# A lead of 224 bytes ahead of all pools of the on-chip memory

## The chip, the cores and the metric

One core of a Trainium2 chip. The metric is the device time of one execution in microseconds, as the median of several runs; lower is better. Each of the core's engines (TensorE, VectorE, ScalarE, GpSimd, SyncE) has its own queue of instructions and they wait for one another by semaphores. Sixteen DMA engines move data between the device's main memory and the on-chip memory (128 partitions; an address below is a byte within a partition, the same in all of them).

## The reference

One inference step of a decoder layer: a matrix-memory branch (mLSTM) and a sliding-window attention branch side by side, merged by gates, with an adaptive norm in front and a final norm. It runs on a prompt of 1024 tokens and on 8 samples of 4 tokens with states and caches. Cut to its main lines, from `layer`, `mlstm_chunk` and `sink_attend`:

```
h = rmsnorm(x, g_norm) * (1 + scale) + shift            # scale, shift, gate = silu(c) @ w_ada + b_ada
(mq, mk, mv, mi, mf, mo, mz, aq, ak, av, az, gm, ga) = split_in(h @ w_in)
# mLSTM branch, chunks of 128 tokens, 4 heads:
s = (q @ k.T) * exp(dmat - m_hat)
num = s @ v + w_inter * (q @ C);  C_new = decay * C + (w_end * k).T @ v
y_m = norm(num / max(|dot|, exp(-m_hat))) * sigmoid(mo) * silu(mz)
# attention branch, window of 128, 8 heads over 2 key heads, with sinks:
p = exp(q @ k.T / 8 - mx);  o = p / (sum(p) + exp(sink - mx)) @ v
y_a = o * silu(az)
u = sigmoid(gm) * (y_m @ w_mo) + sigmoid(ga) * (y_a @ w_ao)
y = rmsnorm(x + gate * (u @ w_o), g_final)
```

Everything is float32. D_MODEL is 1024, the input projection has 5896 columns, and the states, the last keys and values and both outputs are returned.

## The kernel before

The kernel is one program for one core, written by the function `body`. The token axis (1024 + 32) is cut into pieces of 384, 384 and 288 columns, or into halves of 512. Activations are kept transposed, channels on the 128 partitions.

**Start.** `load_x` loads x by channel block: eight tiles of 128 x 512 for each half of the tokens (`x<-xT` in the profile, rows of 2048 bytes a partition), with a tile `small` of constants and samples in between. ScalarE and VectorE square each tile as it lands (`xsq<-x`), TensorE sums the squares (`xs`), and from the sums come the factors of the norm (`xb`). Meanwhile parts of w_ada come in as `early_h`, `early_l` and `adar_q`, from which TensorE works out scale and shift.

**Middle.** Each float32 product of an activation with a weight is made of three products of halves in a reduced format: h is split into `h_h` + `h_l`, a weight tile into `wh` + `wl`, and TensorE adds `wh*h_h`, `wh*h_l` and `wl*h_h`. The jobs `g_ak`, `g_av`, `g_aq`, `g_mq`, `g_mk`, `g_mv` do this for the projections by pieces of 384 or 288 columns; `bw`, `bx`, `by`, `bz` for the gates by 512 columns; `g_w_mo` and `foW` to `foZ` for the output projections. In these products the activation is the moving operand and the weight is loaded into the array ahead (`PEld` in the profile), except in `fo`, where parts of w_out (`wo_...`) move and the tokens are loaded.

A class `Side` fits the attention units (`sc`, `pt`, `oT`) and the chunks of the memory branch (`S`, `U`, `n`, with the running state in the tiles `C`) between these jobs by costs written out in the code, and every instruction of TensorE, VectorE and ScalarE stands in a fixed order. Loads and stores are issued by SyncE in the order of the code, a few by ScalarE and GpSimd. Results that have to change their layout go through main memory (`kD`, `qD`, `oD`, `yaD`, `tmD`, `nmd` and others).

**End.** The last product is added to the rows of x, normalised (`rows_h`, `fy`) and stored (`y_p<-rows_h`).

**Places.** Tiles come from two pools of the on-chip memory, `cp` (lines 176 and 307 on: constants and small tiles) and `sp` (line 177: all else). A pool hands out its tiles one after the other, each rounded up to 32 bytes, and `sp` stands behind `cp`. In `sp` the tag `half` (`ht`, line 193) has 50 buffers of 2048 bytes; `wr`, `wh` and `wl` are weight tiles of 2048 bytes; the activations h and y lie in quarters of 4 x 1056 elements, so that one channel block starts 4224 bytes after the one before.

```
        cp = ctx.enter_context(tc.tile_pool(name="cp", bufs=1))
        sp = ctx.enter_context(tc.tile_pool(name="sp", bufs=1))
...
        def ht(shape, name, dt=F32):
            return sp.tile(shape, dt, tag="half", bufs=50, name=name)
...
        cst = cp.tile([128, C_END], F32, name="cst")
        vec = cp.tile([128, 28], F32, name="vec")
```

Of the kernel before, what the change touches and what calls it, by code (L numbers as in the profile page):

```python
# [10 lines left out]
F32 = mybir.dt.float32  # L11
# [23 lines left out]

C_ID, C_S9, C_TRI, C_CM, C_AM, C_TS, C_CS, C_RS, C_S32, C_BM, C_S64 = 0, 128, 137, 265, 393, 649, 681, 713, 745, 777, 785
C_END = 849


def shape_constants():  # L40
    f = np.float32
    c = np.zeros((128, C_END), f)
    i = np.arange(128)
# [129 lines left out]
def body(tc, a):  # L173
    nc = tc.nc
    with ExitStack() as ctx:
        cp = ctx.enter_context(tc.tile_pool(name="cp", bufs=1))
# [16 lines left out]
        def ht(shape, name, dt=F32):  # L193
            return sp.tile(shape, dt, tag="half", bufs=50, name=name)
# [46 lines left out]
        def dma(out, in_, late=False):  # L241
            stores(in_.tensor)
            issue(out, in_, late)
# [52 lines left out]
        def load_x(p, k0, k1, ts):  # L296
            for k in range(k0, k1):
                ts.append(ht([128, 512], f"x{p}_{k}"))
                dma(ts[-1], a["xT"][:, p, k])
# [4 lines left out]
        issue(small, a["small"])  # L304
        load_x(0, 2, KT, xT[0])
        load_x(1, 0, KT, xT[1])
        cst = cp.tile([128, C_END], F32, name="cst")
        vec = cp.tile([128, 28], F32, name="vec")
        cT, xS = (small[:, o:o + KT * n].rearrange("p (k n) -> p k n", k=KT) for o, n in ((C_TRI + 28, 9), (C_TRI + 28 + KT * 9, NS)))
# [2007 lines left out]
def build(d):  # L2317
    nc = bacc.Bacc("TRN2", target_bir_lowering=False, num_devices=1, dynamic_dma_scratch_size=1024)
    aps = {}
    for k, v in d.items():  # L2320
        aps[k] = nc.dram_tensor(k, v.shape, mybir.dt.from_np(v.dtype), kind="ExternalInput").ap()
    for k, s in OUTS.items():
        aps[k] = nc.dram_tensor(k, s, F32, kind="ExternalOutput").ap()
    with tile.TileContext(nc) as tc:
        body(tc, aps)
    return nc
# [19 lines left out]
```

## Time and profile before

| | |
|---|---|
| median of 3 runs | 842.34 us (842.21 to 842.41) |
| the profiled execution | 842.49 us, span 840.7 us, mean granted clock 0.997 |
| busy: TensorE, its weight loads | 819.6 us (97% of the span), 666.8 us (79%) |
| busy: VectorE, ScalarE, GpSimd | 599.2 us (71%), 421.7 us (50%), 66.2 us (8%) |
| moved by DMA | 153.96 MB in 106690 packets, mean 183 GB/s |

The profile is of one execution. Times of rows are in microseconds unless marked ns. "x12" is the number of instructions in a row, `out<-in` names what is written and read, and what stands in brackets or behind an arrow is the idle time ahead and who ended it. The DMA share is of 16 engines and can pass 100% where packets overlap. Rows of the matmuls overlap too, since they are pipelined: what one costs is read from an unbroken piece of many.

### The profile page before, as it was taken

How to read it: one execution, taken by the hardware profiler on the slowest of the kernel's cores; microseconds unless marked ns; L12 is line 12 of the kernel's file. 1: busy time of each engine (PE TensorE's matmuls, PEld its weight loads, DVE VectorE, ACT ScalarE, POOL GpSimd, SP SyncE). 2: the span in 40 equal slices, each digit the busy share in tenths (PEclk: the TensorE clock that was granted, in tenths of full speed). 3: DMA queues.
4: the chain of work that ended last, by engine and by line, in shares of the span. 5: the costliest groups of instructions: out<-in, count | busy, mean ns of one | idle time of the engine just before them, and what ended most of it. 6: DMA issues, size and time to landing. Idle time of an engine off the chain costs nothing.

```text
span 840.7 us, 15062 instructions
## 1 busy us (share of the span) xinstructions
PE 819.6 (97%) x5129; PEld 666.8 (79%) x5129; DVE 599.2 (71%) x1501; ACT 421.7 (50%) x1032; POOL 66.2 (8%) x128
## 2 busy tenths in 40 slices
PE   6999999999999999999999999999999999999996
PEld 3779897888788788887788877777777779997775
DVE  4889886656655555656657776787878988974776
ACT  5664365655475464445464545344545654334342
POOL 0120000000000000000000100000002104250000
PEclk9999999999999999999999999999999999999998
DMA  9997756356445333579735433553345685643532
GB/s 334 374 355 232 201 184 202 117 155 210 138 135 170 104 115 93 179 247 321 261 131 186 139 124 118 166 177 127 126 149 189 210 288 183 205 138 127 200 108 106
DMA packets 106690, 153.96 MB, mean 183 GB/s; under 512 B 20449, under 2 KB 54369, under 8 KB 106581
## 3 DMA queue, kind: packets, MB, share of 16 engines
q1 hardware_dynamic: 100964, 142.25, 51.9%
q10 hardware_dynamic: 4176, 6.56, 2.2%
q0 software_dynamic: 1472, 4.20, 1.3%
q8 instruction: 40, 0.66, 0.3%
q14 instruction: 38, 0.30, 0.1%
HBM read 109.22 MB, written 44.75 MB: 183 GB/s over the span
## 4 chain that ended last, share of the span: by engine, by line
PE 88%; DMA 5%; DVE 4%; issue 1%; ACT 1%; SPq 0%; DVEq 0%; ACTq 0%
PE bw L258 11%; PE bx L258 11%; PE by L258 10%; PE g_aq L258 6%; PE g_w_mo L258 6%; PE bz L258 5%; PE g_mq L258 3%; PE foW L258 3%; PE foX L258 3%; PE foY L258 2%; PE sc L258 2%; PE oT L258 2%; PE foZ L258 2%; PE smp L258 2%; PE pt L263 2%; PE n L258 2%
## 5 line engine op out<-in xcount | busy, mean ns | idle before, releaser
L219 ACT ACTIVATE p<-p,nmx 128x256 f32<-128x256 f32 (+1 forms) x64 | 31.0, 485 | 10.6 <-DVE nmx L219 10.3
L258 PE MATMUL g_aq<-h_h,wh_aq 128*128 128x384 f32 (+1 forms) x96 | 32.5, 338 | 0.0
L219 DVE CUSTOM_DVE_ANT_0 p<-sc,cst,sink 128x256 f32<-128x256 f32 (+1 forms) x64 | 26.2, 464 | 8.3 <-PE sc L258 8.2
L258 PE MATMUL g_w_mo<-ym_l,wh_w_mo 128*128 128x384 f32 (+1 forms) x96 | 31.1, 324 | 0.0
L258 PE MATMUL g_aq<-h_l,wh_aq 128*128 128x384 f32 (+1 forms) x96 | 31.0, 323 | 0.0
L258 PE MATMUL g_w_mo<-ym_l,wl_w_mo 128*128 128x384 f32 (+1 forms) x96 | 31.0, 323 | 0.0
L258 PE MATMUL g_aq<-h_h,wl_aq 128*128 128x384 f32 (+1 forms) x96 | 31.0, 323 | 0.0
L258 PE MATMUL g_w_mo<-ym_h,wh_w_mo 128*128 128x384 f32 (+1 forms) x96 | 31.0, 323 | 0.0
L246 POOL DMA_DIRECT2D oD<-uqv x16 | 8.8, 552 | 202.5 <-ACT uqv L219 172.8
L219 ACT ACTIVATE et<-et,an 128x128 f32<-128x128 f32 x32 | 11.2, 395 | 25.7 <-DVE et L219 21.3
L258 PEld LDWEIGHTS g_aq<-h_h,wh_aq 128*128 128x128 f32 x96 | 18.1, 188 | 2.6 <-issue 1.5
L219 DVE COPY p<-pt 128x512 f32<-128x512 f32 (+1 forms) x16 | 10.5, 655 | 12.3 <-PE pt L263 12.3
L258 PE MATMUL sc<-ukv,uqv 64*128 64x256 f32 (+1 forms) x128 | 18.3, 390 | 0.8 <-DVE p L219 0.8
L258 PEld LDWEIGHTS g_aq<-h_l,wh_aq 128*128 128x128 f32 x96 | 18.1, 188 | 0.0
L258 PEld LDWEIGHTS g_w_mo<-ym_h,wh_w_mo 128*128 128x128 f32 x96 | 18.0, 188 | 0.0
L258 PEld LDWEIGHTS g_w_mo<-ym_l,wh_w_mo 128*128 128x128 f32 x96 | 18.0, 188 | 0.0
L219 ACT ACTIVATE p<-p,den 128x256 f32<-128x256 f32 (+1 forms) x32 | 14.4, 491 | 7.3 <-DVE den L219 7.3
L258 PEld LDWEIGHTS g_aq<-h_h,wl_aq 128*128 128x128 f32 x96 | 18.0, 188 | 0.0
L258 PEld LDWEIGHTS g_w_mo<-ym_l,wl_w_mo 128*128 128x128 f32 x96 | 18.0, 188 | 0.0
L219 DVE TENSOR_TENSOR wor<-wor,gb 128x512 f32<-128x512 f32 x16 | 10.8, 690 | 9.8 <-DMA wor<-w_out 9.7
L258 PE MATMUL g_mq<-h_h,wh_mq 128*128 128x384 f32 (+1 forms) x48 | 16.9, 351 | 0.3 <-ACT mk L219 0.3
L219 ACT ACTIVATE sq<-rows_h 128x512 f32<-128x512 f32 (+2 forms) x14 | 8.2, 583 | 17.8 <-issue 12.0
(2078 smaller groups left out, 2858.7 us busy)
## 6 DMA issues: line engine op xcount, KB each, us to landing
x<-xT SPq DMA_DIRECT2D x16, 256.0 KB, 5.4
early_h<-w_ada SPq DMA_DIRECT2D x8, 512.0 KB, 9.0
adar_ga<-w_ada SPq DMA_DIRECT2D x16, 256.0 KB, 4.3
wr_ga<-w SPq DMA_DIRECT2D x16, 256.0 KB, 2.9
wr_gm<-w SPq DMA_DIRECT2D x16, 256.0 KB, 3.5
taD<-gt SPq DMA_DIRECT2D x16, 256.0 KB, 2.0
tmD<-gt SPq DMA_DIRECT2D x16, 256.0 KB, 4.4
wor<-w_out SPq DMA_DIRECT2D x16, 256.0 KB, 6.6
```

Source lines behind the costliest of these rows:

```text
L219: ins = f(*args, **kw)
L246: ins = (eng or nc.sync).dma_start(out, in_)
L258: in_order(nc.tensor.matmul(out, lhsT, rhs, start=start, stop=stop, skip_group_check=more))
L263: in_order(nc.tensor.transpose(out, in_, idn))
```

## The change

Ahead of the first tile of `cp`, a tile of 56 float32 per partition (224 bytes) is asked for. Nothing writes or reads it.

```diff
 C_END = 849
+LEAD = 56
...
         load_x(1, 0, KT, xT[1])
+        cp.tile([128, LEAD], F32, name="lead")
         cst = cp.tile([128, C_END], F32, name="cst")
```

All tiles of both pools begin 224 bytes later. The places of some, from the allocation lists of the two built programs (first byte, and its distance past a multiple of 256):

```
tile                        before         after
cst (constants)              1152  128      1376   96
one                          5728   96      5952   64
x, first half, block 0      16928   32     17152    0
wr_ak                      119328   32    119552    0
early_h                    137760   32    137984    0
wh_ak                      188704   32    188928    0
h_l, channel block 0       205088   32    205312    0
h_l, channel block 1       209312  160    209536  128
C, its six buffers         222272 to 224992 (64, 96, 128, 160, 192, 224)
                           222496 to 225216 (32, 64, 96, 128, 160, 192)
```

Of the 1491 places of tiles on the chip 1486 move, all by 224; 1255 then begin on a multiple of 256, and 1254 of them began 32 bytes past one. The order of the instructions on every engine and their number are the same. The tiles in the matrix unit's result memory and in main memory stay where they are.

## The prediction

> **What bounds the kernel now.** I read the page first, for the shares of the engines over the span.
>
> ```profile
> span 840.7 us, 15062 instructions
> PE 819.6 (97%) x5129; PEld 666.8 (79%) x5129; DVE 599.2 (71%) x1501; ACT 421.7 (50%) x1032; POOL 66.2 (8%) x128
> ...
> PEclk9999999999999999999999999999999999999998
> DMA  9997756356445333579735433553345685643532
> ```
>
> TensorE is busy for 97% of the span at nearly full granted clock. That leaves 840.7 - 819.6 = 21.1 us without a matmul. The DMA engines are full only in the first slices. The second view is the list of waits, for TensorE alone: what does it wait for in those 21 us?
>
> ```profile
> PE xc L258 <- ACT xsq L219: 6.4, 1, 6.4
> PE S L258 <- DVE C L219: 1.4, 1, 1.4
> PE bw L258 <- DVE wor L219: 0.8, 1, 0.8
> ```
>
> One wait of 6.4 us at the very start, and then nothing over 1.4 us. The rest of the 21 us is mostly the end, behind the last matmul. So a change of addresses can move the time in three places: at the start, where the first matmuls hang on loads; at the end, where the last rows are normalised and stored; and inside the 5129 matmuls, if the place of an operand changes what one of them takes. The third view is the timeline of the start.
>
> ```profile
> 1.65 0.43 SPq L246 DMA_DIRECT2D small<-small  x1
> 2.12 8.90 SPq L246 DMA_DIRECT2D x<-xT  x14
> 5.93 0.42 ACT L219 ACTIVATE xsq<-small 128x256 f32<-128x256 f32 x1 [3.91 <-DMA small<-small]
> 10.04 0.63 ACT L219 ACTIVATE xsq<-x 128x512 f32<-128x512 f32 x1 [0.73 <-DMA x<-xT]
> 10.70 2.06 DVE L219 TENSOR_TENSOR xsq<-x 128x512 f32<-128x512 f32 x3 [0.66 <-DMA x<-xT]
> 12.53 0.58 ACT L219 COPY xsum<-xs 128x512 f32<-128x512 f32 x1 [1.87 <-PE xs L258]
> 13.02 3.74 ACT L219 ACTIVATE xsq<-x 128x512 f32<-128x512 f32 x6
> 17.78 1.49 PE L258 MATMUL xb<-xdg,one 128*128 128x128 f32 x10
> ```
>
> The squares of the first half of x wait for each load in turn, until the last of them starts at 10.70 us. From 13.02 us ScalarE does six squares back to back (3.74 us for 6, with no wait in the row), so there the loads no longer lead. What a load saves by 10.70 us is saved by all that follows; what it saves later is not.
>
> **The change, part by part.** No instruction is added, taken out or moved: the order on each engine is word for word that of before, apart from buffers' numbers. The unused tile of 224 bytes is placed ahead of all others, and every tile of the two pools starts 224 bytes later. The large ones began 32 bytes past a multiple of 256 and now begin on one. Distances between tiles stay as they were. The allocation lists of the two built programs show this for 1486 of 1491 places; the five that stay are four constants and a scratch area. A rival in which the change does nothing to the addresses is thereby out.
>
> *Transfers.* What does a row of a transfer cost, and how much of that can hang on its first address? Two stretches at full load, one of rows of 2048 bytes (x), one of 4096 (w_ada), each with the DMA view:
>
> ```profile
> DMA packets 639, 1.16 MB, mean 386 GB/s; under 512 B 73, under 2 KB 73, under 8 KB 639
> q1 hardware_dynamic: 639, 1.16, 103.1%
> ```
>
> ```profile
> DMA packets 554, 2.03 MB, mean 406 GB/s; under 512 B 60, under 2 KB 60, under 8 KB 553
> q1 hardware_dynamic: 553, 2.02, 102.1%
> ```
>
> The first is 8 to 11 us, with 639 - 73 = 566 large packets in 103.1% of 16 engines x 3 us: 87.4 ns each. The second is 26 to 31 us, with 553 - 60 = 493 in 102.1% of 16 x 5 us: 165.7 ns each. So 2048 bytes more cost 78.3 ns, and about 9 ns of a row are fixed. A row that begins 32 bytes late touches one block of 256 bytes more. All it can gain is the fixed part, 9 ns of 87 (10%); it need not gain anything. I take the price of the 32 bytes that stick out, 78.3 x 32 / 2048 = 1.2 ns (1.4%), because the second 2048 bytes, with their eight block borders, run at the plain rate: a border as such is not dear.
>
> The Trainium skill (DMA: Bandwidth & Descriptors, "How a descriptor splits into AXI transactions") has a row that starts off a multiple of 256 begin with a transaction at the border below. By it a row of 2048 bytes goes from 9 transactions and 65 beats to 8 and 64, an estimate of 1.5% from that page's figures. Its price alone would take the start 0.1 us down, as mine does. No run so far has large rows that start on a multiple, so the trace cannot confirm it.
>
> At the start, the loads that lead run from 2.12 to 10.70 us, 8.6 us. 1.4% of that is 0.12 us; the ends are 0 and 10%, 0.9 us. Later loads are waited for by VectorE and ScalarE alone:
>
> ```profile
> DVE et L219 <- DMA et<-nmd: 13.3, 6, 4.5
> DVE wor L219 <- DMA wor<-w_out: 9.7, 6, 4.0
> ACT wh_w_mo L219 <- DMA wr_w_mo<-w_mo: 7.1, 3, 4.2
> ```
>
> These 30 us are fifteen waits for whole transfers of some 4 us. At 1.4% each would shorten by 0.06 us, and TensorE's own list above shows that it has other matmuls meanwhile (its one wait for wor is 0.8 us). I cost them at nothing; with the cover gone they are worth 30.1 x 1.4% = 0.4 us. SP's queue issues the same transfers in the same order, so nothing is passed. At the end:
>
> ```profile
> 835.54 0.75 DVE L219 SCALAR_TENSOR_TENSOR rows_h<-rows_h,fy,rows_l 128x512 f32<-128x512 f32 x1
> 836.29 0.40 ACTq L246 DMA_DIRECT2D y_p<-rows_h  x1
> ```
>
> The last store is issued at 836.29 us; of the 4.4 us to the end its 128 rows over 16 engines take 8 x 87.4 ns = 0.7 us. 1.4% of that is 0.01 us, 10% 0.07 us.
>
> *Engines.* What a start address does to an instruction can be read only from tiles that already lie at several distances from a multiple of 256. The six buffers of C lie 64, 96, 128, 160, 192 and 224 bytes past one; the blocks of hv 32, 36 and 40 bytes past.
>
> ```profile
> L258 PE MATMUL n<-hv,et 128*128 128x129 f32 x64 | 12.1, 281 | 0.0
> L258 PE MATMUL n<-C,qw 128*128 128x129 f32 x56 | 10.8, 275 | 0.0
> L258 PE MATMUL U<-hv,hk 128*128 128x129 f32 x64 | 9.2, 275 | 0.0
> ```
>
> With C the mean is 275 ns, and with hv 275 and 281 ns for the same form. Nothing there follows the distance from 256 by more than the 6 ns between the two hv rows, which have the same starts. But none of these tiles starts on a multiple, and the matmuls that fill the span are others. They are found in the chain of waits, in unbroken pieces:
>
> ```profile
> 345.65 2.77 PE bw L258 x12
> ...
> 804.16 4.08 PE foW L258 x18
> ```
>
> The same form (512 columns) takes 2.77 / 12 = 231 ns with h as the moving operand and 4.08 / 18 = 227 ns with w_out's parts. So matmuls of one form do differ by some 4 ns with operand and stage. Whether the place in memory has a part in it the trace does not say. I take 0 for the shift, by the C row, which is the only one over many starts, and because every distance between two tiles stays. The bounds are a quarter of the 4 ns either way: 1 ns x 5129 = 5.1 us faster or slower. This is the one term that can move the time by more than a few tenths, and 0.2% (1.7 us, about what a measurement of this kernel can tell from no change) needs only 1.7 / 5129 = 0.33 ns a matmul.
>
> The Trainium skill (SBUF — State Buffer, "Specifications (TRN2)") gives the memory lines of 16 bytes and charges for crossing to a new one. Starts at 32 and at 0 past a multiple of 256 are both at the beginning of such a line; by it the engines gain nothing from this change and the sum is the transfers' alone. The C row agrees (starts all multiples of 16, one mean of 275 ns), but does not cover a start on 256.
>
> *Sum.* The profiled execution took 842.49 us beside the median of 842.34, 0.15 more, with a span of 840.7 (1.8 us lie around it). Start -0.12, middle 0, end -0.01, matmuls 0: 842.49 - 0.13 = 842.36 for that execution, and 842.2 against the median.
>
> **The rivals.** *Faster: the matmuls gain.* A moving row of 1536 or 2048 bytes that starts 32 past a multiple touches seven or nine blocks of 256 bytes, and one that starts on it six or eight. If the read pays for blocks, each matmul is a little shorter. For it: 231 ns for 512 columns is not the floor for the form, as the 227 ns show. Against it: the 227 ns are reached by tiles that start 32 bytes past a multiple as well, and h's rows, 4224 bytes apart, end up on a multiple only for every other row. At 0.65 ns a matmul, the middle between 0.33 and the bound of 1 ns, it gives 842.3 - 3.3 = 839.0; at the bound 837.2. The start alone (0.9 us at most) cannot reach 0.2%.
>
> *Slower: the border moves to the start of the stream.* Now a block's border lies 224 bytes into each row, with the stream running; after the change the weights' load and the moving read both begin on a border, where nothing has been read ahead. PEld is busy for 666.8 us beside PE's 819.6, so the two run side by side almost always. If they meet at their first block, each matmul pays. For it: TensorE is the bound, and nothing hides it. Against it: weights and half the moving rows share their distance from a border (32) now, too. It decides from 0.33 ns a matmul on; at 0.65 ns it gives 845.6, at 1 ns 847.4.
>
> **How the numbers follow.** No change that can be measured, 842.2: 0.55, with a range of its own from 841.2 (start at its bound) to 843.0 (0.13 ns a matmul lost). Faster rival 0.25, since fewer blocks can only help the read itself, and the 4 ns between two pieces of one form show that there is something to gain. Slower rival 0.20: it needs a collision that the equal distances speak against, but one third of a nanosecond is little to exclude. The range goes to the middle of the faster case, 839.0, and into the slower one up to 844.5 (0.42 ns), which leaves out about 0.12 + 0.08. Faster by over 0.2% (below 840.7) 0.25, within 0.55, slower (above 844.0) 0.20.
>
> **What would show it.** In the profile after: 8 to 11 us moves its rows of x at some 86 ns instead of 87.4 (if 78, the block price was real); the three squares on VectorE start at about 10.6; bw stays at 2.77 us for 12 and foW at 4.08 for 18. A matmul piece that takes 2.76 or less everywhere, or 2.78 and more, is one of the rivals. If TensorE's busy time stays within 1 us of 819.6 and the time still moves by over 1.7 us, a wait has come or gone that I have not seen, and the prediction's reading of the start or the end is wrong.

## The result, and the profile after

The changed kernel takes 842.26 us (median, 840.75 to 845.46 over 12 runs) beside 842.38 us for the kernel before on the same chip (841.63 to 846.23 over 12). The ratio is 0.9999 with a 95% interval of 0.9984 to 1.0014: no change that can be measured, as forecast. The profiled execution took 841.70 us, with a span of 839.9 us and a granted clock of 0.997. The first rows of its page:

```profile
span 839.9 us, 15062 instructions
PE 818.9 (97%) x5129; PEld 666.5 (79%) x5129; DVE 598.7 (71%) x1501; ACT 421.7 (50%) x1032; POOL 66.8 (8%) x128
```

TensorE's busy time moved from 819.6 to 818.9 us over the same 5129 matmuls. Its list of waits has the same head (a line number is one higher throughout, since a line was added):

```profile
PE xc L259 <- ACT xsq L220: 6.3, 1, 6.3
PE S L259 <- DVE C L220: 1.6, 1, 1.6
```

The two pieces of the chain of waits in which the matmuls were priced, which were 2.77 and 4.08 us before:

```profile
345.97 2.77 PE bw L259 x12
...
803.46 4.08 PE foW L259 x18
```

Neither piece moved by a hundredth of a microsecond. At the left stand their starts: foW came at 804.16 us before and at 803.46 now, so this execution is 0.70 us ahead. That lead comes from the start, in the timeline:

```profile
9.93 1.96 DVE L220 TENSOR_TENSOR xsq<-x 128x512 f32<-128x512 f32 x3 [0.62 <-DMA x<-xT]
...
17.33 1.49 PE L259 MATMUL xb<-xdg,one 128*128 128x128 f32 x10
19.73 1.92 PE L259 MATMUL ada_q<-early_h,c 128*32 128x512 f32 x16
```

The three squares begin at 9.93 us instead of 10.70, the matmuls of xb at 17.33 instead of 17.78, and the first product with w_ada (`ada_q`) at 19.73 instead of 20.19. The DMA view of 8 to 11 us, and then of 26 to 31 us:

```profile
DMA packets 667, 1.21 MB, mean 402 GB/s; under 512 B 78, under 2 KB 78, under 8 KB 667
q1 hardware_dynamic: 667, 1.21, 105.4%
```

```profile
DMA packets 618, 2.07 MB, mean 413 GB/s; under 512 B 68, under 2 KB 68, under 8 KB 617
q1 hardware_dynamic: 617, 2.06, 101.8%
```

The first is 589 large rows in 105.4% of 16 x 3 us, 85.9 ns each beside 87.4. In the second, sizes are mixed, so bytes are compared with the engines' time: 413 GB/s in a share of 101.8% is 406 GB/s of a full share, beside 406 in 102.1%, that is 398, before. Both are some 2% better. Whether that is the addresses or chance is what the first experiments ask.

### The profile page after: what moved, and what is told of

Read it like the earlier page. It is cut to its first block, busy times and chain, and to the rows that moved or that the text cites. A ratio compares the mean times of both kernels' runs of the same rounds, so it can differ in the third digit from the quotient of the medians.

```text
span 839.9 us, 15062 instructions
## 1 busy us (share of the span) xinstructions
PE 818.9 (97%) x5129; PEld 666.5 (79%) x5129; DVE 598.7 (71%) x1501; ACT 421.7 (50%) x1032; POOL 66.8 (8%) x128
## 4 chain that ended last, share of the span: by engine, by line
PE 87%; DMA 5%; DVE 4%; issue 2%; ACT 1%; SPq 1%; DVEq 0%; ACTq 0%
PE bx L259 10%; PE bw L259 10%; PE by L259 9%; PE g_aq L259 6%; PE g_w_mo L259 6%; PE bz L259 5%; PE g_mq L259 3%; PE foW L259 3%; PE foX L259 3%; PE foY L259 2%; PE sc L259 2%; PE foZ L259 2%; PE smp L259 2%; DMA et<-nmd 2%; PE oT L259 2%
## 5 line engine op out<-in xcount | busy, mean ns | idle before, releaser
L220 DVE TENSOR_TENSOR wor<-wor,gb 128x512 f32<-128x512 f32 x16 | 10.6, 688 | 9.1 <-DMA wor<-w_out 7.5
```

The costliest lines, as they stand in the source:

```text
L220: ins = f(*args, **kw)
```

## Experiments

For all of them a time of each matmul from its start to the start of the next was taken from the trace, by matching its records one to one with the program's instructions, over unbroken stretches of matmuls of one kind. "b" are the jobs `bw` to `bz` and `aw` to `az` (512 columns, the weight is loaded). What moves in them is h in 743 of the 1457 intervals below, sums and differences of blocks of h (`t2` to `t4`) in 563, and other activations (`ym`, `ya`) in 151. "fo" is the output projection (512 columns, w_out moves and u is loaded). Before, b takes 230.67 ns (1457 intervals) and fo 227.45 (326); after, 230.64 and 227.41.

### The same two kernels once more

No edit: how much do two executions of one program differ?

> The kernel before, unchanged, for a second profile. Theory A (the 0.7 us that the changed kernel's profile is ahead at the end comes from its transfers at the start): the first product with w_ada stands where it stood, within 0.15 us of 20.19, and rows of x between 8 and 11 us cost 87.4 ns again. Rival B (one execution's chance): it moves by 0.3 us or more from one execution to the next.

> The changed kernel, unchanged, for a second profile. Theory A: the lead at the start repeats, 0.5 to 0.8 us at the first products with w_ada, and the jumps between 250 and 400 us, which come from single transfers, do not repeat. Rival B: the lead at the start is gone or doubled.

The kernel before took 846.07 us this time with a span of 844.3, against 842.49 and 840.7: 3.6 us between two executions of one program. Followed matmul by matmul, the two stay within 0.12 us of each other until 253 us; the difference is 0.55 us at 279, 0.9 at 397, 3.13 at 425 and 3.62 from 449 to the end. The first product with w_ada started at 20.27 us, 0.08 later than in the first profile, as theory A has it. The waits of TensorE in that repetition show one of the places where time was lost, and the stretch around it a second cause:

```profile
PE S L258 <- DVE C L219: 2.6, 1, 2.6
PE bw L258 <- DVE wor L219: 1.1, 1, 1.1
...
397.00:450.00 53.00, 50.42 (x311) 41.69 (x310) 33.18 (x76) 24.43 (x66) 0.31 (x3) 0.97 0.60 199
```

The two waits were 1.4 and 0.8 us. The third line is of the stretch from 397 to 450 us, and its 0.97 is the granted clock, which was 1.00 in the first profile. Right behind the wait for C the clock was 0.75 from 420 to 425 us and 0.91 from 425 to 430, and the matmuls of 512 columns there began 0.43 us apart instead of 0.23. Eight such intervals add 1.6 us, which with the 1.2 us of longer waiting is about the 2.7 lost between 397 and 449 us. Between the start and the last microseconds such a dip occurs in one other profile, that with a lead of 192 bytes (below), and in no third. Over nine of this study's profiles (the two kernels twice, the other leads, the added loads and the wider tiles of 64 bytes, below) the wait for C lies between 0.8 and 2.6 us and that of `sc` between 0.5 and 2.2, in no order of the addresses. The changed kernel took 841.61 us with a span of 839.8, and began xb at 16.95 us, 0.38 earlier than in its first profile. Its first product with w_ada started at 19.35 us, 0.84 ahead of the kernel before, a little over the 0.5 to 0.8 that theory A expected. Two profiles are too few to tell a tenth of a per cent, so the start was tried with other leads.

### Other leads

```diff
-LEAD = 56
+LEAD = 48   # large tiles 224 bytes past a multiple of 256
```

```diff
-LEAD = 56
+LEAD = 24   # large tiles 128 bytes past
```

> A lead of 192 bytes, so that large tiles begin 224 bytes past a multiple of 256. Theory A1 (a row pays for the bytes from the border below it, so 256 for the first 32): a row of x costs 7 ns more than before, 94 to 95 ns, the start is 0.7 us later than before and the whole 0.8 us longer. Theory A2 (a row pays for each block of 256 bytes that it touches: nine, as before): 87.4 ns and no difference from before. Rival B (the address does not matter to a row): 87.4 ns too, and the same in the changed kernel. In all of them TensorE's pieces stay, bw at 2.77 us for 12 and foW at 4.08 for 18.

> A lead of 96 bytes, so that large tiles begin 128 bytes past a multiple of 256. Theory A1: half of a block is paid twice, 3.7 ns more for a row of x than before, 91 ns, and the start 0.35 us later. Theory A2 and rival B: as before, 87.4 ns. A third, A3 (only multiples of 64 or 128 count, not 256): as the changed kernel, about 86 ns, with the start 0.5 to 0.7 us ahead of before.

224 bytes past a multiple: 843.86 us, ratio to the kernel before 0.9999 (0.9978 to 1.002). 128 bytes past: 843.23 us, ratio 0.9989 (0.9967 to 1.0012). Neither can be told from no change. The starts of xb, first 224 and then 128 bytes past:

```profile
16.95 1.49 PE L259 MATMUL xb<-xdg,one 128*128 128x128 f32 x10
```

```profile
18.28 1.49 PE L259 MATMUL xb<-xdg,one 128*128 128x128 f32 x10
```

One is as early as the earlier of the two starts on a multiple of 256, the other the latest of all ten profiles with unchanged loads. That a lead which leaves the large tiles off a multiple keeps the start late is thereby refuted, and with it theories A1 (later with both leads) and A3 (earlier with 128 bytes): off a multiple xb starts anywhere from 16.95 to 18.28 us, and the 0.45 us by which the changed kernel led is inside that. The two starts on it, 17.33 and 16.95, lie in the early half; two are too few for more. Nor did a lead at the start always last: that of the first of these two was gone by 69 us.

The price of a row between 8 and 11 us, on which the theories were to be told apart, does not help: it was 89.0 ns with 224 bytes past and 93.9 with 128, but also 94.3 and 94.1 in the kernels with wider h (below), where x lies as in the kernel before.

The stretch of 26 to 31 us tells more. With the leads of 192 and 96 bytes:

```profile
DMA packets 567, 2.03 MB, mean 406 GB/s; under 512 B 62, under 2 KB 62, under 8 KB 566
q1 hardware_dynamic: 566, 2.02, 101.8%
```

```profile
DMA packets 558, 2.03 MB, mean 406 GB/s; under 512 B 63, under 2 KB 63, under 8 KB 557
q1 hardware_dynamic: 557, 2.02, 102.1%
```

Per full share that is 399 and 398 GB/s, as before the change. All eight profiles off a multiple, with the loads unchanged, have 397 to 399; the second one on it has 407. (The two with added loads, where other loads fall into the stretch, have 401 and 404.) So a start on a multiple does seem to bring about 2% here.

The single rows bear this out. Over the whole span the median row of 2048 bytes takes 84 ns in all twelve profiles, and that of 4096 bytes 159 to 161 ns. But that median mixes stretches of all kinds. Of the first 1536 rows of 4096 bytes, the twelve loads of w_ada into `early_h` and `early_l`, 1515 and 1531 take exactly 159 ns in the two profiles on a multiple. In the ten off it only 308 to 639 do, and nearly all others take 160 to 172. Their means are 159.7 and 160.4 ns on a multiple, 163.5 to 164.8 off it, and it makes no difference whether the tiles begin 32, 128 or 224 bytes past one (163.8, 163.7, 163.9). The rows of x show nothing of the kind: of the first 1024 rows of 2048 bytes (x and `small`), in the ten profiles with unchanged loads, 907 and 902 take 84 ns on a multiple, 874 to 915 off it. Why w_ada's rows gain and x's do not is open. The kernel's time does not show the gain.

### h begun 4 and 16 bytes later

The uniform shift leaves open whether starts matter at all to a matmul. So the four quarters that hold h were made 32 bytes a partition wider, and h laid into them 4 bytes (then 16) behind their start:

```diff
-                hs[q] = quarter(q, [128, 4, T], "h", F32R)
+                hs[q] = quarter(q, [128, 4 * T + 8], "h", F32R)[:, 1:4 * T + 1].rearrange("p (k t) -> p k t", k=4)
```

> The kernel before, with the quarters of h begun 4 bytes later, so that every row of the moving operand of the projections and gates starts 36 or 164 bytes past a multiple of 256, off the lines of 16 bytes. Theory A (a matmul minds a start off a multiple of 16 bytes, not one off 256): a few ns for each of some 2900 matmuls with h; at 4 ns 12 us longer, with bw at 2.8 us or more for 12 instead of 2.77. Rival C (a matmul does not mind its start address at all): 842, bw at 2.77.

> The same with 16 bytes instead of 4: starts at 48 or 176 past a multiple of 256, no longer multiples of 32. Theory A: no difference from before, bw 2.77 us for 12. Rival D (lines of 32 or 64 bytes count): as long as with 4 bytes more, by 5 us or over.

With 4 bytes: 851.88 us, ratio 1.0106 (1.0077 to 1.0134). With 16 bytes: 846.87 us, ratio 1.0036 (1.0018 to 1.0054). TensorE's busy time is 829.1 and 824.4 us, 9.5 and 4.8 more than before, beside losses of 8.9 and 3.0 us by the ratios (6.5 to 11.3, 1.5 to 4.5). So the loss is in the matmuls, though with 16 bytes the one profiled execution shows a little more than the many runs. In b, h begun 4 bytes off takes 236.3 ns and 16 bytes off 231.8 (743 intervals each, the same products), so the 4 bytes cost 4.5 ns against 16. Theory A wanted no difference from before with 16 bytes, and rival D as much as with 4; the measured time lies between. What a start costs by itself this edit cannot tell, since h also moves against its weights. The surprise is in matmuls whose own operands were not touched: fo went from 227.45 to 233.4 ns in both. Its operands begin at 32 bytes past a multiple of 64 or at 0, as they did in one kernel or another without harm. What has changed is that the tiles behind the wider quarters moved by 32 to 128 bytes against the others. Hence a new theory: the distance between the moving rows and the loaded weights sets the time.

### h's quarters wider by 32 and by 64 bytes, and nothing else

```diff
-                hs[q] = quarter(q, [128, 4, T], "h", F32R)
+                hs[q] = quarter(q, [128, 4 * T + 8], "h", F32R)[:, :4 * T].rearrange("p (k t) -> p k t", k=4)
```

and the same with `4 * T + 16`.

> The four quarters that hold h are made 32 bytes a partition wider, and are read and written from their first byte: no operand begins off a multiple of 32, but the tiles that lie behind them, the weights above all, move by 32 to 128 bytes against the others. Theory D (a matmul's time hangs on the distance between the start of its moving rows and that of its weights, and a distance of 32 past a multiple of 64 costs some 6 ns): the output projection's matmuls (fo, 512 columns), which begin where they did but stand 32 past a multiple of 64 from their weights, go from 227.4 to about 233.4 ns from start to start, those of the input projections (b, 512 columns) from 230.7 to between 231.5 and 234, and the kernel takes 844.5 to 847.5 us, ratio 1.002 to 1.006. Theory S (each operand's own start counts, by its place against 16 or 32 bytes): nothing begins at a new phase of 32, fo stays at 227.4, b at 230.7, ratio within 0.002 of 1.

> The same four quarters made 64 bytes a partition wider, so that the tiles behind them move by multiples of 64 against the others. Theory D (distance past a multiple of 64): all distances are multiples of 64 again, fo stays at 227.4 plus or minus 0.7 ns, b at 230.7 plus or minus 0.7, and the ratio is within 0.002 of 1. Theory W (any change of the quarters' width or of the places behind them costs, through the places that tiles rotate to): fo is at 232 to 234 again, and the kernel takes 844.5 to 847.5 us, ratio 1.002 to 1.006.

32 bytes wider: 846.81 us, ratio 1.0035 (1.0021 to 1.0049). 64 bytes wider: 844.81 us, ratio 1.0016 (1.0001 to 1.003). The pages, 32 bytes first:

```profile
PE 824.0 (97%) x5129; PEld 666.8 (79%) x5129; DVE 598.7 (71%) x1501; ACT 421.5 (50%) x1032; POOL 66.4 (8%) x128
```

```profile
PE 820.0 (97%) x5129; PEld 666.6 (79%) x5129; DVE 598.5 (71%) x1501; ACT 421.4 (50%) x1032; POOL 67.2 (8%) x128
```

The piece of fo in the chain that took 4.08 us, again 32 bytes first:

```profile
808.44 4.17 PE foW L258 x18
```

```profile
805.24 4.11 PE foW L258 x18
```

By the place of both operands within 64 bytes, the mean intervals are (in brackets how many):

```
kernel           moving, weights      b (512 columns)     fo (512 columns)
before               32, 32           230.67 (1457)       227.45 (326)
after                 0, 0            230.64 (1459)       227.41 (327)
32 bytes wider        0, 0            229.91  (393)
                     32, 32                               229.64  (42)
                     32, 0            233.20 (1062)       234.02 (285)
64 bytes wider       32, 32           231.06 (1457)       229.09 (327)
```

On these means the pair 32, 0 is dear, by 2.5 ns in b and 6.6 in fo, while weights at 0 with moving rows at 0 are harmless in the changed kernel and weights at 32 with moving rows at 32 in the kernel before. So theory S, by which each operand's own start counts, falls. The sum of both kinds covers the change of busy time: 1457 x 1.64 (b's mean of 232.31 over all, less 230.67) + 327 x 6.01 (fo's 233.46 less 227.45) = 4.4 us beside 824.0 - 819.6 = 4.4; the ratio gives 3.0 us (1.8 to 4.1).

Theory D, by which the distance modulo 64 sets the time, holds only in part. Split by what moves, the intervals of b with 32 bytes more are:

```
what moves        before             32 bytes wider     of these at 32, 0
h              231.19 (743)        231.22 (743)      382, at 232.52; the rest 229.83
t2 to t4       230.33 (563)        233.56 (562)      all
others         229.32 (151)        233.25 (151)      118, at 233.74; the rest 231.52
```

In the products of h half of the pairs are at 32, 0, and the sum has not changed: what these intervals gained the others lost. The projections of h in 384 and 288 columns, again half at 32, 0, have hardly changed either (437 intervals at 184.0 ns before and 183.4 after; 220 at 138.0 and 138.1). So the whole loss lies in products that do not read the wider tiles. In `t2` to `t4`, and in the 285 dear intervals of fo, the distance (the moving rows' start less the weights') is 160 modulo 256 throughout. In h, where several distances occur, those of 160 took 3.3 ns longer than the same products before and those of 96 2.7, but those of 32 were 1.4 shorter and those of 224 0.3. Nor is the same place always cheap: the 42 intervals of fo at 32, 32 took 2.8 ns more than the same intervals before. With 64 bytes more b stays within the 0.7 ns that theory D allowed, but fo does not: 229.09 is 1.6 ns up, far from the 232 to 234 of the rival, yet a miss. What is shown is that moving tiles against one another changes such matmuls; which distance counts, and why, is not. The opposite pair (moving at 0, weights at 32) and a distance of 160 alone were not tried.

### More loads ahead of x, and behind it

The prediction held that what a load saves after 10.70 us is not saved. Four loads of 256 KB that nothing reads (the tile's name is new, the data a piece of a weight) were put ahead of x's third tile (the edit shown), then behind its last:

```diff
         issue(small, a["small"])
+        for i in range(4):
+            issue(ht([128, 512], f"more{i}"), a["w1"][20 + i, :, 0:4])
         load_x(0, 2, KT, xT[0])
         load_x(1, 0, KT, xT[1])
```

> The kernel before, with four more loads of 256 KB (parts of the weights, into tiles that nobody reads) put between the first two tiles of x and the other six of its first half. They take 4 x 0.66 = 2.6 us at full load. Theory A (the loads of x that lead are passed on in full to the end): the whole 2.6 us longer (2.0 to 3.2). Rival E (TensorE's own work at the start covers them): under 1 us.

> The same four loads behind the last tile of x, ahead of the parts of w_ada. The prediction's reading (loads behind 10.70 us cost nothing): no difference, under 0.5 us. Rival F (the first product with w_ada waits for its part, though the profile names no transfer ahead of it): 1.5 to 2.6 us longer.

Ahead: 846.22 us, ratio 1.0033 (1.0019 to 1.0048), that is 2.8 us (1.6 to 4.0), and xb starts 2.63 us later than before, as theory A had it (2.0 to 3.2):

```profile
20.41 1.49 PE L258 MATMUL xb<-xdg,one 128*128 128x128 f32 x10
```

Behind: 847.5 us, ratio 1.0048 (1.0035 to 1.0061), that is 4.0 us (2.9 to 5.1). Here xb starts at 17.65 us, as ever, and the loss comes a step later:

```profile
20.05 2.14 PE L258 MATMUL ada_q<-early_h,c 128*32 128x512 f32 x8
22.42 1.05 PE L258 MATMUL ada_q<-early_h,c 128*32 128x512 f32 x4 [0.23 <-DMA early_h<-w_ada]
23.70 1.05 PE L258 MATMUL ada_q<-early_h,c 128*32 128x512 f32 x4 [0.23 <-DMA early_h<-w_ada]
```

In the kernel before, all sixteen ran from 20.19 to 22.34 us with no wait for a load in the row. Now they end at 24.75, 2.4 us later, with the wait for `early_h` written out. So those loads had at most some 0.2 us to spare, and bandwidth up to 22 us is on the path. In the repetition of the kernel before, with its loads unchanged, the weight load of the same product already waits for them:

```profile
21.03 0.25 PEld L258 LDWEIGHTS ada_q<-early_h,c 128*32 128x32 f32 x6 [0.19 <-DMA early_h<-w_ada]
```

The matmul intervals are those of before in both kernels (b 230.66 and 230.74, fo 227.33 in both), so the loss is not in them. At 253 us the two kernels stand 2.6 and 2.8 us behind the one before, and at 571 us 1.9 and 3.1: what was lost at the start stays, but for the scatter of single waits in between. The start explains 2.4 to 2.8 of the 4.0 us behind x (rival F said 1.5 to 2.6); for the rest no cause is shown.

## Why the prediction was right, and where it was not

**Matmuls, 0: right, and for the reason given second.** The row of C gave one mean over six starts, and the prediction added that all distances stay. The second is what carries it. With all tiles shifted together, to 0, 128 and 224 bytes past a multiple, b stays at 230.6 to 230.7 ns and fo at 227.4; with some tiles moved against others, by 32 bytes, fo goes to 233.5 and the sums of h's blocks from 230.3 to 233.6. The row of C was read rightly, but is no guide to those. Split by the six starts it gives 275.2 to 275.7 ns for each, though three of the six lie 32 bytes off their weights modulo 64. So what the products of 512 columns feel these matmuls of 129 columns do not. Of the bounds of 1 ns either way this change used 0.04; for a shift of one pool alone they would have been too narrow.

The prediction's 4 ns between b and fo as a sign "that there is something to gain" misled. The two differ by 3.2 ns at the same pair of places, in the kernel before (32, 32) as in the changed one (0, 0), so this difference is not one of place. Places do have a part elsewhere, up to 6.6 ns, but where distances were kept, as here, there was nothing to gain.

The Trainium skill (SBUF — State Buffer, "Specifications (TRN2)") gives lines of 16 bytes. By it a start at 32 or at 0 is alike, which the shift confirms (227.45 and 227.41 ns for fo). By it a start 4 bytes off should pay; h 4 bytes on is in line with this (236.3 ns against 231.8 at 16 bytes), but the edit changed the distances too. The lines do not account for the 6.6 ns between the pairs, both of whose starts are on lines.

**Faster rival: fell.** Rows that touch one block of 256 bytes less read no faster: b 230.64 ns against 230.67. With large tiles 128 or 224 bytes past, b stays at 230.7 as well.

**Slower rival: fell.** If weights and moving rows that meet at a border cost, the changed kernel would show it, since both are at 0 there. Its matmuls took what they took before (227.41 ns for fo).

**Transfers, 1.4%: seen, but not where it was counted.** A row that starts off a multiple does pay where w_ada is loaded: 163.5 to 164.8 ns for 4096 bytes against 159.7 and 160.4 on it, 2 to 3%, and the stretch of 26 to 31 us gained about 2% (from 397 to 399 GB/s of a full share to 406 and 407, in two profiles on a multiple against eight off it). But the prediction spent the 1.2 ns on the rows of x, whose times show no price at all. The stretch of 8 to 11 us, from which "86 ns" was to be read, cannot decide: it gave 85.9 and 89.4 ns on a multiple of 256, and 87.4 and 87.8 off it for the kernel before. That 85.9 came out as forecast was luck.

The Trainium skill (DMA: Bandwidth & Descriptors, "How a descriptor splits into AXI transactions") would have every row off a multiple pay for the bytes fetched below its start, one beat in 65 at 32 bytes. The rows of w_ada agree that a start off a multiple pays, but not that it pays by the bytes below: 32, 128 and 224 bytes past cost the same (163.8, 163.7 and 163.9 ns). The rows of x, at 84 ns on and off a multiple, do not bear it out.

**Start, -0.12 us: cannot be told.** The three squares began at 9.93 us instead of "about 10.6", and xb 0.45 us earlier. The experiments put xb anywhere from 16.95 to 18.28 us with the loads unchanged. So the sign agreed by chance as far as can be told: x's rows are no cheaper on a multiple, and 0.12 us would drown in a scatter ten times as large, which the prediction did not price.

**Later loads at nothing: the step that failed.** "What it saves later is not" saved was read from six squares in a row at 13.02 us, that is from ScalarE alone. TensorE's next need, `early_h`, comes from the same queue behind x, and 2.6 us of loads there cost 1.0048. For this change it makes little: 1.4% of the 20 us from 2 to 22 us would be 0.28 us instead of 0.12.

**Middle and end, 0 and 0.01: right in sum.** The wait of bw for wor, 0.8 us before, is gone after and was 1.1 us in the repetition of before. Such waits come and go by a microsecond without a change, and a dip of the granted clock can follow one, which is also why a profile's 0.8 us less span here means nothing.

## What to carry to other kernels

A shift of all pools keeps every distance, and none of the three shifts tried here changed a matmul. Moving some tiles against others did. Before padding a tile, ask which other tiles it moves and by how much: 32 bytes added to four tiles cost 0.35% here, in products that never read them. A mean over matmuls of many kinds hides where such a cost sits; compare each product with itself in the other kernel. The same holds for a median over all rows of a transfer size. And a view that says that one engine no longer waits for a queue does not say that nobody does: follow the queue to its next reader before a later load is priced at nothing.

## What was not expected of the hardware

Matmuls of 512 columns whose moving rows and weights begin 32 bytes apart modulo 64 took 233.2 to 234.0 ns from start to start on average, and 227.4 to 231.1 ns where they begin at the same place modulo 64, with every start a multiple of 32. Why is open, and the distance modulo 64 is not the whole rule: the products of h, half of them 32 apart, took 231.2 ns as before. In the kernel with h 16 bytes on, b took 231.2 ns with the weights 16 past the moving rows and 232.5 with 48.

Rows of DMA were 2 to 3% shorter on a multiple of 256 bytes in the loads of w_ada (nearly all of them exactly 159 ns for 4096 bytes), by the same amount against 32, 128 and 224 bytes past it, and no shorter in the loads of x (84 ns for 2048 bytes).

A wait of 2.6 us was followed by some 3.4 us at half the granted clock in one execution of the kernel before. A wait of 2.4 us, with a lead of 96 bytes, was not.
